# Low parts of the two query projections' weights formed on GpSimd instead of VectorE

## The chip, the cores and the metric

The kernel runs on one core of one Trainium2 chip. The metric is the device time of one execution in microseconds (us); a figure for a kernel is the median of several executions. The trace behind the profile comes from one more execution, taken by the hardware profiler. TensorE's granted clock is given as a share of full speed: 1.00 is 2.4 GHz, 0.50 is 1.2 GHz.

## The reference

Four layers run one after the other on 256 tokens of width 1024, in float32: a gated-MLP mixer and a chunked attention, each with a convolutional feed-forward; then an "even" layer (two attentions and a feed-forward) and an "odd" layer, followed by a final norm. The change lies in the odd layer's attention:

```
q, k, v, iq, ik, iw = split(h @ w_in)          # q: 16 heads x 64, k and v: 4 heads x 64
q, k, iq, ik = rope(...)                       # rotation of each half head
score = sum over 8 index heads of iw * relu(iq . ik)
idx   = top_k(score, 64)                       # for each query, 64 keys of the 256
o     = softmax(q . k[idx]) @ v[idx]           # 4 query heads share a key head
x     = x + g_m * (o @ w_out)
```

Behind it the odd layer has a mixture of 8 experts, two for each token, each with gate, up and down matrices of 1024 x 1408.

## The kernel before, in words

**Split weights.** A float32 product is computed as three TensorE products of rounded operands. A weight block `r`, loaded into a tile `raw`, is split by `split` (line 245): ScalarE rounds it to `hi` (tile `wh`, line 261), and VectorE forms the rest, `lo = r - hi` (tile `wl`, line 262). `unit` (line 265) cuts a loaded block of 128 x 2048 into two splits of 128 x 1024. `mm3` (lines 277 to 280) makes the three products: line 278 and line 279 use the weights' high and low parts with the activation's high part, line 280 the weights' high part with the activation's low part. The tags `wh` and `wl` have 4 buffers each, `raw` has 4.

**Token-major projections.** `tok_out` (line 373) multiplies the 256 tokens (two tiles of 128, `m` = 0 and 1) by a weight in units of half the inputs by `cols` outputs. The sums of both token tiles stand in two PSUM banks; after the second unit of a column block `evac` takes them out. For the projections named `m` in the trace there are two such banks (tag `m`).

**The odd layer's attention, `dsa`** (line 1068 on), in the order of the code: `tok_out` of the index queries (`o_iq`); `tok_out` of keys, index key and index weights (`o_ki`), whose evacuation rotates the keys (lines 885 to 901), transposes them (lines 909 and 779) and copies them (lines 910, 782, 784); then the key selection, `choose(1)` and `choose(0)` side by side: scores by TensorE (line 1110), relu by ScalarE (line 1114), weighted sums `sc` by VectorE (lines 1120 and 1122), the causal mask (1125), 8 rounds of "the eight largest, then strike them out" (lines 1129 and 1130), and the mask `sel` (1132 and 1133). Then the values (`o_v`), then `query(0)` and `query(1)`: each is a `tok_out` of two units of `o_q`, that is four splits of 128 x 1024, with an evacuation `ev_q` that rotates (lines 885 to 895), transposes (779) and stores the queries. Then four attention groups, which need the queries and `sel`, the output projection (`wo`), and the experts.

**Order.** Each engine runs its own queue in order. The queues are laid out when the kernel is built, by a list scheduler with estimated durations: what stands first in the code goes first when several instructions are ready, and later ones fill what it takes for gaps. So subtractions of line 262 for `o_q` stand in VectorE's queue before, between and behind the instructions of the selection. GpSimd, before the change, only computes the norms' inverse roots (lines 307, 949, 950), on 128 x 1 tiles.

Of the kernel before, what the change touches and what calls it, by code (L numbers as in the profile page):

```python
# [13 lines left out]
ALU = mybir.AluOpType  # L14
# [144 lines left out]
def tile_net(ctx: ExitStack, tc: tile.TileContext, a: dict, out: bass.AP):  # L159
    nc = tc.nc  # L160
    V, S, G, PE = nc.vector, nc.scalar, nc.gpsimd, nc.tensor
# [14 lines left out]
    def t_keep(tag, n, bufs, dt=F32):  # L176
        return keep.tile([P, n], dt, tag=tag, name=tag, bufs=bufs)

    def t_part(tag, n, bufs, dt=F32):
        return part[0].tile([P, n], dt, tag=tag, name=tag, bufs=bufs)  # L180

    def psd():
        return ps_p.tile([P, 512], F32, tag="d", name="d", bufs=4)
# [7 lines left out]
    def sm(tag, n, bufs=4):  # L191
        return t_keep("s_" + tag, n, bufs)

    def a8(dt=F32):
        return t_keep("a8", 2048, 6, dt)

    def xn_(dt=F32):
        return t_keep("xn", D, 2, dt)
# [43 lines left out]
    turn = [0]  # L242
    fine = [FINE]

    def split(r, where=None):

        n = r.shape[-1]
        if where == "a8":
            t = a8(F32R)
            hi, lo = t[:, 0:n], t[:, 1024:1024 + n]  # L250
        else:
            turn[0] += 1
            if where and turn[0] % 2:
                hi, lo = (t_part(g, 1024, where, F32R)[:, 0:n] for g in ("whx", "wlx"))
            else:
                hi, lo = (t_keep(g, 1024, WB, F32R)[:, 0:n] for g in ("wh", "wl"))
        parts = 2 if fine[0] > 0 and n > 512 else 1
        fine[0] -= 1
        for i in range(parts):
            cs = slice(i * n // parts, (i + 1) * n // parts)  # L260
            S.activation(hi[:, cs], r[:, cs], AF.Copy)  # L261
            V.tensor_tensor(lo[:, cs], r[:, cs], hi[:, cs], op=ALU.subtract)  # L262
        return hi, lo

    def unit(src, k, where=None, loaded=None):

        r = load(src) if loaded is None else loaded
        n = r.shape[-1] // k
        per = k if k * n <= 1024 else -(-k // 2)
        w = []  # L270
        for k0 in range(0, k, per):
            kk = min(per, k - k0)
            hi, lo = split(r[:, k0 * n:(k0 + kk) * n], where)
            w += [(hi[:, i * n:(i + 1) * n], lo[:, i * n:(i + 1) * n]) for i in range(kk)]
        return w

    def mm3(ps, lh, ll, rh, rl, start, stop):
        PE.matmul(ps, lh, rh, start=start, stop=False)  # L278
        PE.matmul(ps, lh, rl, start=False, stop=False)  # L279
        PE.matmul(ps, ll, rh, start=False, stop=stop)  # L280
# [30 lines left out]
    def new_xt():  # L311
        return tuple(a8(F32R).rearrange("p (k t) -> p k t", k=NK) for _ in range(2))
# [56 lines left out]
    def tok_out(xt, src, cols, evac, psx=None, where=None, loaded=(), ready=()):  # L369

        xh, xl = xt
        for c in range(src.shape[0] // 2):
            ps = [(psx or psd)()[:, 0:cols] for _ in range(2)]
            for kh in range(2):
                u = 2 * c + kh
                w = ready[u] if u < len(ready) else unit(src[u], 4, where, loaded[u] if u < len(loaded) else None)
                for m in range(2):
                    ts = slice(m * P, (m + 1) * P)
                    for k in range(4):
                        kk = 4 * kh + k  # L380
                        mm3(ps[m], xh[:, kk, ts], xl[:, kk, ts], *w[k], kk == 0, kk == NK - 1)
            for m in range(2):
                evac(m, c, ps[m])
# [119 lines left out]
    def ada_all(nm):  # L503
        while any(t[0] == nm for t in ada_todo):
            ada_step()
# [251 lines left out]
    def half(t, hd, idx=None):  # L757
        return t[(hd % 2) * 64:(hd % 2) * 64 + 64, hd // 2 if idx is None else idx, :]
# [145 lines left out]
    def tr_copy(src, dst, m, scale=1.0):  # L904

        n = src.shape[1] // P
        ps = pst()
        for c in range(n):
            PE.transpose(ps[:, c * P:(c + 1) * P], src[:, c * P:(c + 1) * P], ident)
        S.activation(dst[:, :, m * P:(m + 1) * P], ps[:, 0:n * P].rearrange("p (k t) -> p k t", k=n),  # L910
                     AF.Copy, scale=scale)
# [167 lines left out]
    def dsa():  # L1079
        xt = ahead[2]  # L1080
        ib, kk = a8(), a8(F32R)
        oT = new_xt()
        ikT = ib[:, 0:256].unsqueeze(1)
        iw = ib[:, 256:272].rearrange("p (m d) -> p m d", m=2)
        iqT = ib[:, 512:1536].rearrange("p (k t) -> p k t", k=4)
        sel = t_part("sel", 512, 1, F32R).rearrange("p (m t) -> p m t", m=2)
        kh, kl = (kk[:, i * D:(i + 1) * D].rearrange("p (k t) -> p k t", k=4) for i in range(2))
        vv = ib[:, 1536:2048].rearrange("p (m d) -> p m d", m=2)
        def ev_iq(m, c, ps):
            tr_copy(rotate(ps, m, 8), iqT, m)  # L1090

        tok_out(xt, a["o_iq"], 512, ev_iq)

        def ev_ki(m, c, ps):
            tr_copy(rotate(ps[:, 256:320], m, 1, dup=2), ikT, m)
            V.tensor_scalar(iw[:, m, :], ps[:, 320:328], float(8 ** -0.5 * 64 ** -0.5), None, op0=ALU.mult)
            stack(rotate(ps[:, 0:256], m, 4, dup=2), m, kh, kl)

        tok_out(xt, a["o_ki"], 328, ev_ki)

        def choose(m):

            nk = (m + 1) * P
            sc = t_part("sc", T, 2)[:, 0:nk]
            first = True
            for h0 in (0, 1, 4, 5):
                ps = psd()
                for i in range(2):
                    hd = h0 + 2 * i
                    PE.matmul(ps[:, i * nk:(i + 1) * nk], half(iqT, hd)[:, m * P:(m + 1) * P],  # L1110
                              half(ikT, hd, 0)[:, 0:nk], start=True, stop=True)
                yield
                rl = t_part("pT", 512, 4)
                S.activation(rl[:, 0:2 * nk], ps[:, 0:2 * nk], AF.Relu)
                yield
                for i in range(2):
                    hd = h0 + 2 * i
                    r1, w1 = rl[:, i * nk:(i + 1) * nk], iw[:, m, hd:hd + 1]
                    if first:
                        V.tensor_scalar(sc, r1, w1, None, op0=ALU.mult)  # L1120
                    else:
                        V.scalar_tensor_tensor(sc, r1, w1, sc, op0=ALU.mult, op1=ALU.add)
                    first = False
                yield
            V.tensor_tensor(sc[:, m * P:], sc[:, m * P:], m_caus, op=ALU.add)
            yield
            for _ in range(8):
                mx = sm("top", 8)
                V.max(mx, sc)
                V.match_replace(sc, mx, sc, -3e38)  # L1130
                yield
            V.tensor_scalar(sel[:, m, 0:nk], sc, -3e38, NEG, op0=ALU.not_equal, op1=ALU.mult)
            V.tensor_tensor(sel[:, m, m * P:nk], sel[:, m, m * P:nk], m_caus, op=ALU.add)

        def ev_v(m, c, ps):
            S.activation(vv[:, m, :], ps, AF.Copy)

        qs = []

        def query(c, ready=()):  # L1140
            for _ in range(2):
                q = xn_(F32R) if c == 0 else t_part("qs", D, 2, F32R)
                qs.append(q.rearrange("p (k t) -> p k t", k=4))

            def ev_q(m, _, ps):
                for o, q in zip(rotate(ps, m, 8, parts=True), qs[2 * c:]):
                    stack(o, m, q, scale=0.125)

            tok_out(xt, a["o_q"][2 * c:2 * c + 2], 512, ev_q, psm, ready=ready)

        def group(g, psx):
            attend(stacked(qs, kh, kl, 0, lambda hd: g), lambda hd, kb: vv[:, kb, g * 64:(g + 1) * 64],
                   None, oT, g, psx,
                   rmask=lambda m: sel[:, m, 0:(m + 1) * P])

        ada_all("o")
        rows_out("o", mod_scale("o", 4, "o_norm_ffn_2"))
        together(choose(1), choose(0))
        tok_out(xt, a["o_v"], 256, ev_v, psm)
        query(0)  # L1160
        g_m = spread("o", 2)
        ready = [unit(a["o_q"][2 + u], 4) for u in range(READY)]
        for step in ORD:
            if step == "q":
                query(1, ready)
            else:
                group(int(step), psd if step in PSD else psm)
        plan()
        out_proj(oT, a["wo3"], g_m)
# [293 lines left out]
```

## Time and profile before

| | before |
|---|---|
| median of 3 runs | 1533.95 us (1530.49 to 1535.28) |
| profiled execution | 1537.47 us |
| its span in the trace | 1535.5 us |
| mean granted TensorE clock | 0.981 |
| busy: TensorE matmuls, VectorE, ScalarE, GpSimd | 1460.7, 1219.9, 932.1, 16.5 us |

The span runs from the first to the last instruction of the trace; the profiled execution took 1.97 us more than its span, and 3.5 us more than the median of the runs without a profile. Busy times are sums over the whole span; a stage has to be read from its own windows.

### The profile page before, as it was taken

The numbers are of one execution on the slowest core, as the hardware profiler recorded it, in microseconds if no ns is written. First come the engines' busy times: TensorE is split into PE (matmuls) and PEld (weight loads), VectorE is DVE, ScalarE is ACT, GpSimd is POOL, SyncE is SP. The second block draws the span as 40 slices with busy tenths as digits, with TensorE's granted clock in tenths as the row PEclk, the third lists the DMA queues.
The fourth block names the chain that finished last, engine by engine and source line by source line (L and its number), as shares of the span: only waits on it lengthen the run. The fifth ranks groups of instructions, "written<-read, shape, count | busy, mean of one in ns | idle before, by whom it ended". The sixth has DMA issues, their size and how long they took to land.

```text
span 1535.5 us, 23191 instructions
## 1 busy us (share of the span) xinstructions
PE 1460.7 (95%) x8916; PEld 1284.8 (84%) x8916; DVE 1219.9 (79%) x2074; ACT 932.1 (61%) x1559; POOL 16.5 (1%) x26
## 2 busy tenths in 40 slices
PE   6999999999999999899899999989799999999996
PEld 5889998899899889788699998778688888888875
DVE  7589887776698777776898875886788889888996
ACT  7656555555575546565654443545577777777774
POOL 0000000000000000000000000000000000000000
PEclk9999999999999999999999999999899999999999
DMA  8658666454387664262488881431489988899894
GB/s 311 218 195 325 226 244 219 149 199 162 134 295 281 220 219 165 83 255 105 164 329 329 322 309 63 180 138 34 152 319 332 335 328 320 319 346 332 294 352 155
DMA packets 55148, 363.05 MB, mean 236 GB/s; under 512 B 6526, under 2 KB 6886, under 8 KB 16630
## 3 DMA queue, kind: packets, MB, share of 16 engines
q1 hardware_dynamic: 55030, 361.50, 65.3%
q8 instruction: 72, 1.18, 0.3%
q14 instruction: 46, 0.38, 0.1%
HBM read 360.37 MB, written 1.10 MB: 235 GB/s over the span
## 4 chain that ended last, share of the span: by engine, by line
PE 82%; DVE 8%; ACT 5%; DMA 4%; issue 1%; POOL 0%; SPq 0%; POOLq 0%; ACTq 0%; DVEq 0%
PE d L278 12%; PE d L279 12%; PE d L280 12%; PE m L279 10%; PE m L280 9%; PE m L278 9%; PE t L280 2%; PE t L279 2%; PE t L278 2%; DMA raw<-in_fin_dram 2%; PE d L745 1%; DVE wl L262 1%; PE t L323 1%; PE t L734 1%; PE t L1259 1%
## 5 line engine op out<-in xcount | busy, mean ns | idle before, releaser
L262 DVE TENSOR_TENSOR wl<-raw,wh 128x1024 fp32r<-128x1024 f32 (+4 forms) x342 | 363.1, 1069 | 71.8 <-ACT wh L261 70.4
L261 ACT ACTIVATE wh<-raw 128x1024 fp32r<-128x1024 f32 (+4 forms) x342 | 315.5, 932 | 121.8 <-PE m L280 30.4
L262 DVE TENSOR_TENSOR wlx<-raw,whx 128x1024 fp32r<-128x1024 f32 (+2 forms) x231 | 258.9, 1123 | 46.1 <-ACT whx L261 45.2
L261 ACT ACTIVATE whx<-raw 128x1024 fp32r<-128x1024 f32 (+2 forms) x231 | 224.0, 975 | 59.1 <-PE m L279 17.1
L278 PE MATMUL d<-wh,a 128*128 128x512 f32 (+4 forms) x448 | 167.9, 376 | 8.6 <-ACT a L344 8.6
L279 PE MATMUL d<-wl,a 128*128 128x512 f32 (+4 forms) x448 | 165.9, 372 | 0.4 <-DVE wl L262 0.4
L280 PE MATMUL d<-wh,a 128*128 128x512 f32 (+4 forms) x448 | 165.5, 371 | 0.2
L279 PE MATMUL m<-a,wh 128*128 128x256 f32 x496 | 141.5, 285 | 0.0
L278 PE MATMUL m<-a,wh 128*128 128x256 f32 x496 | 141.4, 285 | 0.0
L280 PE MATMUL m<-a,wl 128*128 128x256 f32 x496 | 141.3, 285 | 0.0
L500 DVE SCALAR_TENSOR_TENSOR raw<-raw,silu_c 128x1024 f32<-128x1024 f32 x96 | 116.0, 1218 | 4.5 <-DMA raw<-in_e_ada_dram 2.9
L278 PE MATMUL d<-a,th 128*128 128x512 f32 x264 | 107.2, 406 | 6.7 <-ACT th L565 6.6
L279 PE MATMUL d<-a,th 128*128 128x512 f32 x264 | 105.4, 399 | 0.0
L278 PEld LDWEIGHTS d<-wh,a 128*128 128x128 f32 x448 | 86.5, 193 | 22.6 <-ACT a L344 10.9
L261 ACT ACTIVATE a<-raw 128x1024 fp32r<-128x1024 f32 (+1 forms) x72 | 70.0, 986 | 53.1 <-PE d L280 48.1
L279 PE MATMUL d<-wlx,a 128*128 128x512 f32 (+2 forms) x272 | 99.8, 367 | 1.1 <-DVE wlx L262 1.1
L278 PE MATMUL d<-whx,a 128*128 128x512 f32 (+2 forms) x272 | 99.7, 367 | 0.6 <-ACT a L669 0.6
L262 DVE TENSOR_TENSOR a<-raw,a 128x1024 fp32r<-128x1024 f32 (+1 forms) x72 | 81.0, 1132 | 23.7 <-ACT a L261 23.5
L280 PE MATMUL d<-a,tl 128*128 128x512 f32 x264 | 99.6, 404 | 0.0
L280 PE MATMUL d<-whx,a 128*128 128x512 f32 (+2 forms) x272 | 99.4, 365 | 0.0
L279 PEld LDWEIGHTS d<-wl,a 128*128 128x128 f32 x448 | 86.6, 193 | 13.1 <-DVE wl L262 1.6
L280 PEld LDWEIGHTS d<-wh,a 128*128 128x128 f32 x448 | 86.0, 192 | 13.3 <-DVE a L347 1.9
(367 smaller groups left out, 3499.6 us busy)
## 6 DMA issues: line engine op xcount, KB each, us to landing
raw<-in_fin_dram SPq DMA_DIRECT2D x66, 1024.0 KB, 5.1
raw<-in_x_dn_dram SPq DMA_DIRECT2D x40, 1024.0 KB, 6.4
raw<-in_fdn_dram SPq DMA_DIRECT2D x33, 1024.0 KB, 5.1
raw<-in_x_gate_dram SPq DMA_DIRECT2D x32, 1024.0 KB, 6.2
raw<-in_x_up_dram SPq DMA_DIRECT2D x32, 1024.0 KB, 6.8
raw<-in_e_ada_dram SPq DMA_DIRECT2D x24, 1024.0 KB, 5.6
raw<-in_o_ada_dram SPq DMA_DIRECT2D x24, 1024.0 KB, 7.1
raw<-in_wo_dram SPq DMA_DIRECT2D x16, 1024.0 KB, 5.7
```

The costliest lines, as they stand in the source:

```text
L261: S.activation(hi[:, cs], r[:, cs], AF.Copy)
L262: V.tensor_tensor(lo[:, cs], r[:, cs], hi[:, cs], op=ALU.subtract)
L278: PE.matmul(ps, lh, rh, start=start, stop=False)
L279: PE.matmul(ps, lh, rl, start=False, stop=False)
L280: PE.matmul(ps, ll, rh, start=False, stop=stop)
L323: PE.transpose(ps[:, c * P:(c + 1) * P], src[:, c * P:(c + 1) * P], ident)
L500: V.scalar_tensor_tensor(rr, rr, 1.0, silu_c, op0=ALU.mult, op1=ALU.mult, accum_out=t[:, i:i + 1])
L734: PE.transpose(pt[:, b * P:(b + 1) * P], s2[:, b * P:(b + 1) * P], ident)
L745: PE.matmul(ps[:, i * 64:(i + 1) * 64], pT[:, b * P:(b + 1) * P], vv(hd, kb), start=kb == 0, stop=kb == m)
L1259: PE.matmul(ps, gr[:, m, :], t[:, m, cs], start=i == 0, stop=i == 3)
```

## The change

The engine that forms low parts becomes a variable, `low[0]`, which is VectorE everywhere except while `query` runs its `tok_out`: there it is GpSimd. So the eight subtractions of 128 x 1024 for `o_q` (two units for each `query`, two splits for each unit) are issued to GpSimd. All else, the rounding on ScalarE included, stays where it was in the code.

```
+    low = [V]
...
             S.activation(hi[:, cs], r[:, cs], AF.Copy)
-            V.tensor_tensor(lo[:, cs], r[:, cs], hi[:, cs], op=ALU.subtract)
+            low[0].tensor_tensor(lo[:, cs], r[:, cs], hi[:, cs], op=ALU.subtract)
...
+            low[0] = G
             tok_out(xt, a["o_q"][2 * c:2 * c + 2], 512, ev_q, psm, ready=ready)
+            low[0] = V
```

## Rows read from the trace of the kernel before

**Rows 1.** First lines of the page: busy time, share of the span, instructions.
```profile
PE 1460.7 (95%) x8916; PEld 1284.8 (84%) x8916; DVE 1219.9 (79%) x2074; ACT 932.1 (61%) x1559; POOL 16.5 (1%) x26
```
**Rows 2.** Busy us by window; last columns: granted clock, DMA share, GB/s.
```profile
1002.60:1006.20 3.60, 3.57 (x8) 2.84 (x9) 3.60 (x5) 0.00 (x0) 0.00 (x0) 0.50 0.34 84
...
1150.00:1200.00 50.00, 50.00 (x241) 42.06 (x240) 43.80 (x49) 39.01 (x48) 0.00 (x0) 1.00 0.93 333
```
**Rows 3.** What TensorE waited for, 975 to 1023: us, times, longest.
```profile
PE m L279 <- DVE wl L262: 6.4, 1, 6.4
```
**Rows 4.** Timeline of TensorE: start, duration, line, op, tiles, shape, count.
```profile
981.73 0.27 PE L909 MATMUL t<-cst,rt 128*128 128x128 f32 x1
...
990.18 0.40 PE L278 MATMUL m<-wh,a 128*128 128x512 f32 x1
...
995.65 0.61 PE L278 MATMUL m<-wh,a 128*128 128x512 f32 x2
1002.63 0.80 PE L279 MATMUL m<-wl,a 128*128 128x512 f32 x1 [6.37 <-DVE wl L262]
...
1003.65 0.63 PE L278 MATMUL m<-wh,a 128*128 128x512 f32 x1
1004.08 0.63 PE L279 MATMUL m<-wl,a 128*128 128x512 f32 x1
...
1022.24 0.40 PE L280 MATMUL m<-wh,a 128*128 128x512 f32 x1
```
**Rows 5.** Timeline of VectorE over the selection and the first query evacuation.
```profile
978.66 1.22 DVE L262 TENSOR_TENSOR wl<-raw,wh 128x1024 fp32r<-128x1024 f32 x1
979.79 0.75 DVE L901 TENSOR_TENSOR rt<-rt 128x256 f32<-128x256 f32 x2
...
980.91 0.36 DVE L901 TENSOR_TENSOR rt<-rt 128x64 f32<-128x64 f32 x2
...
983.86 1.22 DVE L262 TENSOR_TENSOR wl<-raw,wh 128x1024 fp32r<-128x1024 f32 x1
...
991.22 0.42 DVE L1129 MAX8 s_top<-sc 128x8 f32<-128x256 f32 x1
...
1001.35 1.23 DVE L262 TENSOR_TENSOR wl<-raw,wh 128x1024 fp32r<-128x1024 f32 x1
1002.48 0.30 DVE L1133 TENSOR_TENSOR sel<-sel,cst 128x128 fp32r<-128x128 f32 x1
...
1007.18 0.69 DVE L885 TENSOR_TENSOR rt<-m,cos 128x512 f32<-128x512 f32 x1 [0.42 <-PE m L280]
...
1008.12 0.41 DVE L887 TENSOR_TENSOR rt<-m,sin 128x256 f32<-128x256 f32 x1
```
**Rows 6.** Timeline of ScalarE: roundings of `o_q`, and the index key's copy.
```profile
977.10 2.01 ACT L261 ACTIVATE wh<-raw 128x1024 fp32r<-128x1024 f32 x2 [1.26 <-PE d L280]
...
981.01 1.06 ACT L261 ACTIVATE wh<-raw 128x1024 fp32r<-128x1024 f32 x1 [1.74 <-PE m L280]
...
982.45 0.27 ACT L910 ACTIVATE a<-t 128x128 f32<-128x128 f32 x1
...
990.66 1.05 ACT L261 ACTIVATE wh<-raw 128x1024 fp32r<-128x1024 f32 x1
```
**Rows 7.** Timeline, GpSimd beside VectorE, early and in the even layer.
```profile
42.30 0.15 DVE L304 TENSOR_SCALAR s_ms<-s_ms 128x1 f32<-128x1 f32 x1
...
42.37 1.22 DVE L262 TENSOR_TENSOR wl<-raw,wh 128x1024 fp32r<-128x1024 f32 x1
...
42.53 1.46 POOL L307 TENSOR_TENSOR s_r<-s_ms,mhalf 128x1 f32<-128x1 f32 x1 [29.06 <-DVE s_ms L304]
...
621.73 0.55 POOL L950 TENSOR_TENSOR s_r<-s_ms,mhalf 128x1 f32<-128x1 f32 x1 [194.07 <-DVE s_ms L945]
621.84 0.69 DVE L452 TENSOR_TENSOR h<-h,d 128x512 f32<-128x512 f32 x1 [0.26 <-PE d L280]
```
**Rows 8.** What the DMA queue waited for, 980 to 1035.
```profile
SPq L239 <- DVE wl L262: 32.2, 4, 12.2
```

## Prediction

> **What bounds the kernel now.** I read the page first: TensorE is busy for 95% of the span, VectorE for 79%, and GpSimd for 1% [rows 1]. That only says who has room on average. The windows say where the time is lost: among the experts, which fill the span from about 1100 on, TensorE is busy for 50.00 of 50 us at full clock [rows 2], so what is gained ahead of them should move them forward as a block, and nothing that this change does can shorten them. Next I read the list of waits around the key selection. It has one large entry: TensorE stood 6.4 us for line 279, which reads a low part, until VectorE had made it [rows 3].
>
> The timelines show how that came about. TensorE began the first query projection at 990.18, finished its first unit (24 products, 0.228 us apart), issued two more at 995.65, and then stood until 1002.63 [rows 4]. The low part that it wanted is the one VectorE made at 1001.35; its rounded half had been ready since ScalarE's instruction at 981.01 ended, at 982.07 [rows 5, 6]. So the subtraction was ready 19 us before it ran: it stood in VectorE's queue behind the selection, whose eight rounds start at 991.22 and whose last instruction ends at 1002.78 [rows 5]. The stall has a second price. Behind it the granted clock is 0.50, that is 1.2 GHz, until 1006.2 [rows 2], and products come 0.43 us apart instead of 0.228 [rows 4]: nine of them, 9 x 0.20 = 1.8 us. Together 6.4 + 1.8 = 8.2 us is what this place could give at most.
>
> **The change part by part.** It takes eight subtractions off VectorE and puts them on GpSimd. Two of them stand ahead of the selection, at 978.66 and 983.86, one at 1001.35 inside its last instructions, the rest behind [rows 5].
>
> *TensorE without the stall.* The third low part can be formed from 982.07 on, long before it is wanted at 996.1 (995.65 and two products). The first query's two units then end at 996.1 + 22 x 0.228 = 1001.1. The next query's products need the PSUM bank of the first, which is free when VectorE has rotated out of it: from the start of line 885 to the end of line 887 took 1007.18 to 1008.53, 1.35 us [rows 5]. VectorE comes to that when the selection is over: 1002.78, less 1.13 us for the subtraction at 1001.35, less what the two early ones give back. They took 1.13 us each, but the selection's start hangs on ScalarE and TensorE as well (ScalarE's copy of the index key came at 982.45, behind a rounding that started at 981.01 [rows 6]), so I count 0.8 of 2.3 us. The bank is free at 1002.78 - 1.13 - 0.8 + 1.35 = 1002.2, and TensorE waits 1.1 us for it: the stall does not vanish, it moves to "rotation behind selection". Gain so far 8.2 - 1.1 = 7.1, say 7 us.
>
> *What a subtraction costs on GpSimd.* The trace has none. The nearest rows: from below VectorE's own, 1.22 us; from above, GpSimd's 128 x 1 operation takes 0.55 us where VectorE's takes 0.15 us [rows 7], and 0.55 / 0.15 x 1.22 = 4.5 us. The ends are far apart; I take their geometric mean, 2.35 us, which is an estimate. At that price GpSimd's queue is never late: the first three are done by about 985 to 988, the others follow ScalarE's roundings, which come when TensorE has released a buffer. The Trainium skill, GPSIMD Engine Reference, section 3.1, measures a two-input operation on 128 x 2048 at 4497 ns on GpSimd against 2293 ns on VectorE, and advises VectorE for such work; half of it, 2.25 us as an estimate, would make the sum below 0.2 us better, and no run here shows it.
>
> *GpSimd and VectorE side by side.* This is where the gain can leak. GpSimd's 128 x 1 operation, 0.55 us elsewhere, took 1.46 us when a subtraction with two SBUF operands ran on VectorE from 42.37 to 43.59: it ended 0.40 us after that. Beside an instruction of VectorE that has one operand in PSUM it took 0.55 us [rows 7]. So GpSimd is held up by such an instruction. Whether VectorE is held up while GpSimd streams, no row shows, since GpSimd never streamed. Bounds: below, VectorE never waits, 0 us. Above, each of the three subtractions that fall between 978 and 986 stops it for its whole length: the first starts at 978.1, when its rounding ends [rows 6], and stops the pair of line 901 that now comes at 978.7; the second and third stop the next ones, among them the index key's pair at 980.91 [rows 5], on which the selection hangs. That is 3 x 2.35, less the 1.13 us that line 262 took there before, less 0.45 us of slack (the transposed key was there at 982.0, its copy came at 982.45 [rows 4, 6]): 5.5 us. I take two of three, since VectorE's rotations alternate between PSUM and SBUF operands and the third can fall beside the former: 2 x 2.35 - 1.13 - 0.45 = 3.1, say 3 us later for the selection and for TensorE, whose score products and all behind them move with it. The fourth rounding comes at 990.66 [rows 6], so the later subtractions fall into the eight rounds, whose instructions read one tile; there I count nothing. The Trainium skill, SBUF — State Buffer, section "Who interferes with whom", says that a VectorE instruction with two SBUF inputs and a GpSimd instruction that reads SBUF exclude each other for the whole instruction, whichever comes first. Rows 7 agree for the one direction; by that rule the delay of 3 us stands, and without it the sum would be 7 us.
>
> *Clock.* TensorE would idle about 3 us ahead of the scores. Whether the clock then falls as it did behind 6.4 us I can't read; I take no cost, and 1.8 us as the other end.
>
> *Queues and waits.* GpSimd's queue holds nothing else here (the next inverse root comes behind the output projection). The DMA queue waited for line 262 four times, 32.2 us in all [rows 8], to refill `raw`; it now waits for GpSimd, which is done with the later units earlier than VectorE was, and the loads concerned (`wo`) are wanted only behind the attention groups.
>
> **Sum.** 8.2 - 1.1 - 3.1 = 4.0 us faster. The profiled execution would take 1537.5 - 4.0 = 1533.5 us; the runs without a profile have their median 3.5 us below it, so I forecast 1533.95 - 4.0 = 1530.0 us.
>
> **Rivals.**
>
> *B, VectorE is not held up.* Only GpSimd waits, as in rows 7. Gain 7 us: 1527.0, with 1525.5 to 1528.5 from the slot wait and the two early subtractions. For it: the only direction that the trace shows. Against it: something shared that stops one side.
>
> *C, GpSimd is slow.* At 4.5 us a subtraction, two held-up places give 2 x 4.5 - 1.6 = 7.4 us, gain -0.4: 1534.4; with a third 1538.9. Decides from 4.3 us on. For it: the ratio of the small operations. Against: that ratio is of fixed costs.
>
> *D, the selection's rounds are held up too; slower.* If the largest-eight and strike-out instructions are stopped as well, the three subtractions that become ready in 991 to 1000 (fourth to sixth) each add 2.35 us to a chain of VectorE on which the next bank hangs: 7.05 us more, 4.0 - 7.05 = 3 us slower, 1537.0. It turns to a loss when 1.7 of the three are waited for in full. Against it: these instructions read one tile from SBUF, as does the one in rows 7 that held nothing up.
>
> *E, given back.* The block of the experts doesn't move forward, because its weights come no sooner: the DMA engines are at 0.93 there [rows 2]. 1533.95. Against: TensorE has no gap in that window.
>
> **How the numbers follow.** Chances: forecast 0.45, B 0.25, C 0.10, D 0.12, E 0.08. A change under 0.3%, 4.6 us, can't be told from none here. Faster by more: nearly all of B (0.24), a third of the forecast's case (0.16), 0.02 of the rest: 0.42. Slower by more: half of D, half of C, 0.01 of E: 0.12. Within: 0.46. The range runs from B's best, 1525.5, to between C and D, 1535.5; the upper half of C and D, a sliver of B and the spread of a median lie outside, under 0.2. The likeliest case alone has 1528.5 to 1531.5.
>
> **What would show it.** Right: eight subtractions on GpSimd of some 2.35 us; no 6.4 us wait for a low part; a wait of about 1 us for a PSUM bank at the second query's start; a full clock between 1000 and 1006; instructions of line 901 on VectorE that last 1 to 2 us longer; scores some 3 us later; attention groups 4 us earlier. B: line 901 unchanged and the groups 7 us earlier. C: subtractions over 4 us. D: stretched lines 1129 and 1130. Wrong altogether if the scheduler lays VectorE's or TensorE's queue out in another order, so that the selection moves or queries are rotated inside it.

## The result, and the profile after

| | before | after |
|---|---|---|
| median of 7 runs, side by side | 1533.95 us (1530.49 to 1538.36) | 1541.45 us (1538.87 to 1544.8) |
| profiled execution, its span | 1537.47, 1535.5 us | 1542.14, 1540.3 us |
| mean granted clock | 0.981 | 0.979 |

The ratio is 1.0051, with a 95% interval of 1.0035 to 1.0066: slower by half a per cent, outside the predicted range and of the other sign. Lines of `kernel.py` behind the first edit have moved: 262 is 264 now, 885 to 901 are 887 to 903, 779 is 781, 1110 is 1112; from 1132 on, 1132 is 1134.

GpSimd's timeline after (start, duration, line, operation, tiles, shape, count) shows the eight subtractions at some 2.4 us each, and that they come in two groups: two ahead of the scores, six from 995 on.

```profile
975.36 4.86 POOL L264 TENSOR_TENSOR wl<-raw,wh 128x1024 fp32r<-128x1024 f32 x2 [18.22 <-ACT wh L263]
995.15 2.48 POOL L264 TENSOR_TENSOR wl<-raw,wh 128x1024 fp32r<-128x1024 f32 x1 [14.93 <-ACT wh L263]
999.57 2.41 POOL L264 TENSOR_TENSOR wl<-raw,wh 128x1024 fp32r<-128x1024 f32 x1 [1.94 <-ACT wh L263]
1003.45 4.83 POOL L264 TENSOR_TENSOR wl<-raw,wh 128x1024 fp32r<-128x1024 f32 x2 [1.47 <-ACT wh L263]
1008.89 2.42 POOL L264 TENSOR_TENSOR wl<-raw,wh 128x1024 fp32r<-128x1024 f32 x1 [0.61 <-ACT wh L263]
1013.64 2.39 POOL L264 TENSOR_TENSOR wl<-raw,wh 128x1024 fp32r<-128x1024 f32 x1 [2.33 <-ACT wh L263]
```

VectorE's timeline after: read the durations against the same instructions of before. The rotation's pair on 128 x 256 took 0.75 us [rows 5] and takes 4.60; line 1134 (the mask) takes 3.67 for two, which took 0.29 and 0.23 before; line 891 takes 1.47 and 2.75 where line 889 took 0.69 on average before. Each overlaps a row of the fence above.

```profile
975.90 4.60 DVE L903 TENSOR_TENSOR rt<-rt 128x256 f32<-128x256 f32 x2
...
1004.70 3.67 DVE L1134 TENSOR_SCALAR sel<-sc 128x256 fp32r<-128x256 f32 x2
...
1010.39 1.47 DVE L891 TENSOR_TENSOR rt<-rt 128x512 f32<-128x512 f32 x1
...
1013.83 2.75 DVE L891 TENSOR_TENSOR rt<-rt 128x512 f32<-128x512 f32 x1
```

The eight rounds between them are not stretched, though two subtractions run beside them. VectorE's groups by line, 970 to 1020 us (busy us, then mean ns; 421 ns is the mean before as well):

```profile
L1131 DVE MAX8 s_top<-sc 128x8 f32<-128x256 f32 x8 | 3.4, 421 | 0.0
```

What TensorE waited for, 960 to 1100 us (us in total, times, longest): the 6.4 us wait for a low part [rows 3] is gone, and three others stand in its place: that for `s` of line 897 (the queries' parts) was 1.7 us before, those for `rt` of line 903 (the keys) and of line 889 (a PSUM bank that the rotation still reads) are new.

```profile
PE t L781 <- DVE s L897: 4.5, 4, 2.1
PE t L781 <- DVE rt L903: 3.5, 1, 3.5
...
PE m L280 <- DVE rt L889: 1.5, 1, 1.5
```

TensorE's timeline after, from the last product of the key projection to the router behind the attention:

```profile
974.77 0.31 PE L282 MATMUL d<-wh,a 128*128 128x328 f32 x1
...
980.65 1.08 PE L781 MATMUL t<-cst,rt 128*128 128x128 f32 x4 [3.52 <-DVE rt L903]
...
983.37 3.09 PE L1112 MATMUL d<-a 64*128 64x256 f32 x10
986.39 1.11 PE L781 MATMUL t<-cst,rt 128*128 128x128 f32 x4
...
987.65 5.82 PE L1112 MATMUL d<-a 64*128 64x256 f32 x22
...
997.96 0.40 PE L280 MATMUL m<-wh,a 128*128 128x512 f32 x1
...
1098.17 0.60 PE L1245 MATMUL m<-pk,cst 128*128 128x8 f32 x2 [2.68 <-DVE pk L1215]
```

And the clock in windows at the 3.52 us hole, as the time in which TensorE stood is called below, and behind it (the column behind the busy times):

```profile
977.00:981.00 4.00, 0.48 (x4) 0.39 (x3) 4.00 (x7) 0.00 (x0) 3.22 (x2) 0.84 0.72 301
981.00:984.00 3.00, 3.00 (x14) 2.68 (x13) 2.42 (x8) 0.87 (x2) 0.00 (x0) 0.50 0.92 317
...
992.00:996.00 4.00, 4.00 (x18) 3.68 (x17) 3.52 (x13) 2.10 (x4) 0.85 (x1) 0.50 0.86 263
996.00:1000.00 4.00, 4.00 (x24) 3.65 (x24) 4.00 (x21) 1.71 (x3) 2.06 (x2) 0.91 0.06 26
```

TensorE stood 3.52 us for the keys' rotation, and its clock was then 0.50 from 981 to 996, though it was busy without a gap. The last 22 score products took 5.82 us; where the clock was 1.00 (run e2 below) 22 of them took 3.09.

Three marks on TensorE's timeline make the account, since they hold in every run: A, the last 128 x 328 product; B, the first 128 x 512 product of the queries; C, the first product behind the wait for `pk`. Before, A and C are

```profile
977.65 0.31 PE L280 MATMUL d<-wh,a 128*128 128x328 f32 x1
...
1094.15 0.59 PE L1241 MATMUL m<-pk,cst 128*128 128x8 f32 x2 [2.68 <-DVE pk L1211]
```

and B is at 990.18 [rows 4]. So A to B was 12.53 us and is 997.96 - 974.77 = 23.19: 10.66 us lost ahead of the queries. B to C was 103.97 and is 100.21: 3.76 us gained behind it. Together 6.9 us slower in this stage. In these two profiles A itself stands 2.9 us earlier after the change, and what follows C takes 0.8 us longer, so the span is only 4.8 us longer.

### The profile page after: what moved, and what is told of

Its sections match the earlier page's. It is cut to its first block, busy times and chain, and to the rows that moved or that the text cites. A ratio compares the mean times of both kernels' runs of the same rounds, so it can differ in the third digit from the quotient of the medians.

```text
span 1540.3 us, 23189 instructions
## 1 busy us (share of the span) xinstructions
PE 1464.8 (95%) x8916; PEld 1287.1 (84%) x8916; DVE 1221.6 (79%) x2066; ACT 933.3 (61%) x1559; POOL 36.0 (2%) x34
## 4 chain that ended last, share of the span: by engine, by line
PE 81%; DVE 8%; ACT 5%; DMA 4%; issue 1%; POOL 0%; SPq 0%; POOLq 0%; ACTq 0%; DVEq 0%
PE d L280 12%; PE d L281 12%; PE d L282 12%; PE m L281 9%; PE m L282 9%; PE m L280 9%; PE t L282 2%; PE t L281 2%; PE t L280 2%; DMA raw<-in_fin_dram 1%; PE d L747 1%; PE t L325 1%; PE t L736 1%; DVE wl L264 1%; PE t L1263 1%
## 5 line engine op out<-in xcount | busy, mean ns | idle before, releaser
L264 DVE TENSOR_TENSOR wl<-raw,wh 128x1024 fp32r<-128x1024 f32 (+4 forms) x334 | 353.4, 1066 | 72.4 <-ACT wh L263 71.2
L282 PEld LDWEIGHTS d<-wh,a 128*128 128x128 f32 x448 | 85.7, 191 | 13.1 <-DVE a L349 1.6
L280 PEld LDWEIGHTS m<-a,wh 128*128 128x128 f32 x496 | 94.7, 191 | 1.8 <-issue 0.7
```

The costliest lines, as they stand in the source:

```text
L264: low[0].tensor_tensor(lo[:, cs], r[:, cs], hi[:, cs], op=ALU.subtract)
```

## The experiments

Theory C: a subtraction on GpSimd holds some of VectorE's instructions for its whole length, and what TensorE waits for is late by that. Rival O: the list scheduler laid the queues out in another order (the first key transposes of line 781 now stand behind 16 value products on TensorE instead of 24, and ScalarE rounds the third block behind the scores), and the order costs the time. All marks are in one table; the medians of before, in the same sessions, were 1533.4 (e1 to e4), 1533.35 (e5 to e8) and 1533.98 (e9 to e12). Marks come from the one profiled execution of each run, times from 6 to 12 executions; the profiled one of e7 was the slowest of its twelve; u0 and u1 are the first query's two units. In all fourteen profiles TensorE does the same 91 products from A to B and the same 534 from B to C, and what follows C takes 441.1 to 445.5 us (before: 441.3).

| run | median us | ratio to before, 95% | A to B | B to C |
|---|---|---|---|---|
| before | | 1 | 12.53 | 103.97 |
| after | 1541.45 | 1.0051 [1.0035, 1.0066] | 23.19 | 100.21 |
| e1 ghost | 1554.04 | 1.0126 [1.0091, 1.016] | 26.41 | 109.47 |
| e2 memset | 1525.35 | 0.9953 [0.9933, 0.9973] | 12.08 | 96.06 |
| e3 quarters | 1530.49 | 0.9987 [0.9967, 1.0008] | 13.92 | 98.93 |
| e4 u0 on VectorE | 1537.1 | 1.0013 [0.9992, 1.0034] | 17.99 | 100.73 |
| e5 same, quarters | 1529.99 | 0.9972 [0.9959, 0.9985] | 13.10 | 101.67 |
| e6 u1 only, quarters | 1533.91 | 0.9999 [0.9983, 1.0015] | 13.10 | 102.54 |
| e7 VectorE, early | 1534.9 | 1.0005 [0.9993, 1.0017] | 12.08 | 105.37 |
| e8 product in PSUM | 1536.44 | 1.0014 [0.9998, 1.0029] | 11.95 | 106.68 |
| e9 u0 in quarters | 1533.26 | 1.0003 [0.9988, 1.0018] | 13.92 | 101.33 |
| e10 u0 whole | 1537.7 | 1.0024 [1.0006, 1.0041] | 23.25 | 98.38 |
| e11 PSUM, quarters | 1534.48 | 1.0002 [0.9986, 1.0019] | 11.96 | 106.90 |
| e12 e5 with PSUM | 1532.4 | 1.0 [0.9985, 1.0016] | 11.98 | 103.63 |

**e1, the contention alone.** VectorE forms all low parts again, and the queues of every engine but GpSimd's are those of the kernel before. GpSimd repeats the eight subtractions into a tile that nothing reads.

```
+            V.tensor_tensor(lo[:, cs], r[:, cs], hi[:, cs], op=ALU.subtract)
+            if low[0] is G:
+                G.tensor_tensor(silu_c[:, cs], r[:, cs], hi[:, cs], op=ALU.subtract)
```

> All low parts are formed on VectorE as before, and every instruction queue but GpSimd's is the one of before; GpSimd forms the eight low parts of o_q a second time, into a tile that nobody reads. Theory C (contention: a streaming GpSimd subtraction and a VectorE instruction with two SBUF operands, or a fast one, keep each other out for a whole instruction): VectorE's rotations ahead of the selection stretch as after the change, some 2 to 4 us in all, the selection and TensorE come later by that, and the execution is 3 to 8 us slower than before. Rival O (order: the loss comes from the new order of the queues, and GpSimd's work itself costs nothing): no difference from before within 1.5 us, and no stretched VectorE instruction.

It took 1.26% longer, 19 to 21 us, far more than the 3 to 8 expected, with nothing changed in the order. VectorE's timeline (262 is 264 here, the lines of the rotation are 4 above those of before): the same pair of rotations takes 5.04 us, a later one 5.07, and a subtraction on VectorE itself takes 3.06 us where it takes 1.22 alone.

```profile
970.59 3.06 DVE L264 TENSOR_TENSOR wl<-raw,wh 128x1024 fp32r<-128x1024 f32 x1
973.57 5.04 DVE L905 TENSOR_TENSOR rt<-rt 128x256 f32<-128x256 f32 x2
...
1016.48 5.07 DVE L899 TENSOR_TENSOR s<-rt,s 128x256 f32<-128x256 f32 x2
```

As after the change, the clock adds to it: TensorE stood 5.9 us for the pair, and behind that its clock was 0.50, in this window for instance:

```profile
980.00:998.00 18.00, 18.00 (x67) 15.24 (x66) 12.54 (x41) 7.14 (x15) 0.30 (x1) 0.50 0.45 148
```

**e2, the order alone.** TensorE's, VectorE's, ScalarE's and SP's queues are those of after. GpSimd fills the low part with zeros instead of subtracting, so the low parts of the query weights are left out of the result.

```
+            if low[0] is V:
+                V.tensor_tensor(lo[:, cs], r[:, cs], hi[:, cs], op=ALU.subtract)
+            else:
+                G.memset(lo[:, cs].bitcast(F32), 0.0)
```

> The queues of TensorE, VectorE, ScalarE and the DMA queue are those of after the change; in place of each of the eight subtractions GpSimd writes zeros into the low part, which reads nothing from SBUF (so the low parts of the query weights are left out of the result). Theory C: the pair of rotations (line 903) takes 0.75 us instead of 4.60, TensorE's 3.5 us wait ahead of the key transposes shrinks below 1 us, the clock stays at 1.00 through the scores, and the execution is 4 to 8 us faster than before, 12 to 15 us faster than after. Rival O: the transposes stand ahead of the value products all the same, so it is as slow as after, some 7 us slower than before.

8 us faster than before. O falls as the cause: in the very order of after, the stage is 8.4 us shorter than before, and the clock is 1.00 from 970 to 1000. Timelines of e2, GpSimd's first, then VectorE's (the fill is also shorter than a subtraction and doesn't wait for ScalarE, so this is a bound for the idea, not a version of it):

```profile
975.96 0.95 POOL L267 MEMSET wl<- 128x1024 f32 x1 [2.62 <-PE m L284]
...
995.21 0.95 POOL L267 MEMSET wl<- 128x1024 f32 x1 [0.41 <-PE m L284]
```

```profile
976.54 0.76 DVE L906 TENSOR_TENSOR rt<-rt 128x256 f32<-128x256 f32 x2
...
993.24 0.42 DVE L1137 TENSOR_SCALAR sel<-sc 128x256 fp32r<-128x256 f32 x2
...
995.68 0.69 DVE L894 TENSOR_TENSOR rt<-rt 128x512 f32<-128x512 f32 x1
```

The pair at 976.54 starts beside a fill and takes its usual 0.76 us, and the sum at 995.68 starts beside another and takes its usual 0.69: GpSimd's writes hold neither, its reads did. (The mask at 993.24 has no fill beside it; 0.42 us for two is its length undisturbed.)

**e3, the same work in smaller pieces.** Queues of after; each subtraction on GpSimd is cut into four of 128 x 256.

```
+            k = 1 if low[0] is V else 4
+            for p in range(k):
+                ps_ = slice(cs.start + p * (cs.stop - cs.start) // k, cs.start + (p + 1) * (cs.stop - cs.start) // k)
+                low[0].tensor_tensor(lo[:, ps_], r[:, ps_], hi[:, ps_], op=ALU.subtract)
```

> As after the change, with the same queues on the other engines, but each GpSimd subtraction is cut into four of 128 x 256. Theory C: an exclusion lasts only as long as one instruction, some 0.65 us, so the pair of line 903 takes 1.5 to 2.5 us instead of 4.60, TensorE's hole ahead of the key transposes is 0.5 to 1.5 us, and if that leaves the clock at 1.00 the execution is between 5 us faster and 1 us slower than before. Rival O: as slow as after, about 7 us slower than before, since the order is the same.

Some 11 us faster than after, and not to be told from before. GpSimd works longer (0.84 us a piece on average, 3.3 us a subtraction), but an instruction of VectorE now waits for a piece: the pairs take 1.36 and 1.77 us in place of 4.60, TensorE's holes at line 784 are 0.27 and 0.75 us, and the clock stays at 1.00.

**e4 and e5, the first unit back on VectorE.** Its two subtractions stand on VectorE, the other six on GpSimd; whole in e4, in quarters (the loop of e3) in e5.

```
-            low[0] = G
+            low.extend(([V, V, G, G], [G, G, G, G])[c])
...
-            low[0].tensor_tensor(lo[:, cs], r[:, cs], hi[:, cs], op=ALU.subtract)
+            (low.pop(0) if low else V).tensor_tensor(lo[:, cs], r[:, cs], hi[:, cs], op=ALU.subtract)
```

> The first unit's two low parts go back to VectorE, the other six stay on GpSimd; ahead of the selection the queues are those of before. Theory C: no stretched rotation ahead of the selection, no hole, the clock at 1.00 until the queries, and the 6.4 us wait for a low part gone; but the two sel instructions (line 1134) and the query rotations (line 891) still stretch by 3 to 5 us in all. Faster than before by 0 to 5 us. If the loss sat in the later six subtractions instead: slower than before by 3 us or more.

> The first projection's first unit (two subtractions) stays on VectorE, the other six go to GpSimd, each cut into four of 128 x 256. Theory C (a whole subtraction on GpSimd holds VectorE for its length; a piece holds it for a piece's length): the stretched instructions of the earlier run of this order with whole subtractions (the rotation's pair 1.93 us, the selection's two 2.23 and 2.33 us) fall to under 1.3 us, TensorE has no hole over 0.6 us ahead of the scores, the clock is at 0.9 or more from 980 to 1010, and the kernel takes 1527 to 1531 us, 3 to 7 us faster than before. Rival O (the order of the queues decides): the same as with whole subtractions, 1535 to 1539 us.

e4 misses its gain: one subtraction still fell beside the rotation's pair (1.93 us), TensorE had a hole of 0.93 us, and the clock was 0.76, 0.50 and 0.72 in the three windows of 5 us from 980. In quarters the hole is 0.52 us, the clock is 1.00 from 965 to 1000, and e5 is the one complete version whose interval lies below 1: 0.28% faster, at the edge of what can be told, and the best of several that were tried. It can't be told from e3 (0.9967 to 1.0008).

**e6, only what stood behind the selection.** The second unit's two subtractions of the first query go to GpSimd in quarters, the rest stays on VectorE (`[V, V, G, G], [V, V, V, V]`).

> Only the two subtractions that stood behind the selection (the second unit of the first projection) go to GpSimd, in quarters; the other six stay on VectorE. Theory C: with two subtractions in small pieces there is little to hold; the 6.4 us wait for a low part is gone or moved to a bank wait under 3 us, and the kernel takes 1527 to 1531 us. Rival O: whatever stands on GpSimd, the time follows the place of the key transposes in TensorE's queue; where that is as in the kernel before, the gain ahead of the scores is nothing and only the stall behind the selection changes, 1530 to 1534 us.

The 6.4 us wait is gone, and the time is as before: a miss for C. In its place TensorE waits 2.0 us for the mask, 1.3 us for a PSUM bank, and runs at a clock of 0.80 to 0.86 from 1000 to 1010.

**e7, no GpSimd at all.** The first query's two units are split on VectorE ahead of the selection, and the value projection is moved ahead of it too.

```
-            low[0] = G
+            low[0] = V
...
+        tok_out(xt, a["o_v"], 256, ev_v, psm)
+        first = [unit(a["o_q"][u], 4) for u in range(2)]
         together(choose(1), choose(0))
-        tok_out(xt, a["o_v"], 256, ev_v, psm)
-        query(0)
+        query(0, first)
```

> Nothing on GpSimd: the first projection's two units are split on VectorE ahead of the selection instead of behind it. Theory C: the stall of 6.4 us was a matter of VectorE's order alone, so it goes without contention: no instruction of VectorE is stretched, the low parts are there when TensorE wants them, the bank wait behind the selection is 0 to 3 us, and the kernel takes 1526 to 1531 us, about as the run in which GpSimd only fills with zeros (1525.35). Rival: the two or three subtractions set ahead of the selection (1.13 to 1.3 us each) make the selection and the rotations later by as much, and the gain is under 3 us, 1531 to 1535 us.

No gain, as the rival had it. The stall for a low part is gone; the selection starts 15.72 us behind A in place of 13.57, its mask holds TensorE for 2.8 us and the bank for 1.1, and the clock is 0.50 from 1005 to 1010. Here, moving the subtractions earlier on VectorE only moved the stall; how much of the delay is the value projection's, no run tells.

**e8, which instructions are held.** Whole subtractions on GpSimd, but the rotation keeps its first product in PSUM, so that its sum has one operand in SBUF and one in PSUM. (The scheduler's order is another one again.)

```
-        V.tensor_tensor(hv(t1), hv(ps), bc(rope["cos"], 0, 64), op=ALU.mult)
...
+        V.tensor_tensor(hv(ps), hv(ps), bc(rope["cos"], 0, 64), op=ALU.mult)
+        t1 = ps
```

> The changed kernel, whole subtractions on GpSimd, but the rotation keeps its first product in PSUM, so that none of its instructions reads two operands from SBUF. Theory C by operands (only an instruction of VectorE with two SBUF operands, or the fast one-operand form, is held while GpSimd reads SBUF): the rotation's last two instructions take under 1 us each though GpSimd streams beside them, TensorE's hole ahead of the scores is under 1 us, the clock stays up there, the two instructions that form the mask are still stretched to 2 us or more, and the kernel takes 1527 to 1536 us, at least 5 us less than the changed kernel. Rival (any VectorE instruction is held): the pair still takes over 2.5 us and the time stays at 1539 to 1544 us.

Timelines of e8, GpSimd's and then VectorE's:

```profile
973.75 7.05 POOL L264 TENSOR_TENSOR wl<-raw,wh 128x1024 fp32r<-128x1024 f32 x3 [18.27 <-ACT wh L263]
...
996.05 4.69 POOL L264 TENSOR_TENSOR wl<-raw,wh 128x1024 fp32r<-128x1024 f32 x2 [0.66 <-ACT wh L263]
```

```profile
974.05 0.75 DVE L905 TENSOR_TENSOR rt<-d,rt 128x256 f32<-128x256 f32 x2
...
978.00 0.75 DVE L905 TENSOR_TENSOR rt<-d,rt 128x256 f32<-128x256 f32 x2
978.84 2.30 DVE L1124 TENSOR_SCALAR sc<-pT,a 128x256 f32<-128x256 f32 x2
...
996.21 4.62 DVE L1136 TENSOR_SCALAR sel<-sc 128x256 fp32r<-128x256 f32 x2
```

Both pairs lie inside GpSimd's 7.05 us and take 0.75 us each: with one operand in PSUM nothing is held. The hole ahead of the scores is gone, the clock is 1.00 from 975 to 995, A to B is 11.95 us. What is still held is the form with one SBUF tile and a scalar, lines 1124 and 1136: 2.30 us for two of the weighted sums, 4.62 us for the two of the mask, and TensorE stood 5.2 us for it.

The Trainium skill, SBUF — State Buffer, section "Who interferes with whom", says that VectorE contends with GpSimd's reads when it has two SBUF inputs, and with GpSimd in some fast forms of one input, among them `tensor_scalar`; that others do not contend; and that the blocked side waits for the whole instruction. These rows agree: 4.60 us against 0.75 for the same pair by where its operand lies, 4.62 us against 0.42 for the mask, 421 ns against 421 for the eight largest, 0.76 us beside a fill that reads nothing. No row has a fast form beside a fill.

**e9 and e10, the loss in two parts.** Queues of after. In e9 only the two subtractions ahead of the scores are cut in quarters, in e10 only the other six. (`[4, 4, 1, 1], [1, 1, 1, 1]` and `[1, 1, 4, 4], [4, 4, 4, 4]` pieces.)

> The changed kernel with the first unit's two subtractions alone (those ahead of the selection) in quarters; the other six stay whole, and all queues but GpSimd's are those of the changed kernel. It splits the loss: in the changed kernel's trace the hole ahead of the scores is 3.5 us and the half clock behind it costs the scores 8.91 - 4.76 = 4.2 us and the products around them 1.4 us, 9.1 us together; behind the selection the held instructions cost 1.5 + 2.8 us of waits. Theory C with the clock: hole under 1.1 us, clock at 0.9 or more from 977 to 1000, 7 to 9 us less than the changed kernel, 1532 to 1535 us. Rival (the half clock is not the hole's doing, or the time comes back at the selection): under 4.5 us less, 1537 us or more.

> The complement: the first unit's two subtractions whole, the other six in quarters. Theory C with the clock: the hole of some 3.5 us ahead of the scores and the half clock behind it stay, the mask's two instructions fall from 3.67 us to under 1.5 us, and the kernel takes 1537 to 1540 us, 2 to 4 us less than the changed kernel. Rival as in the run before: 4.5 to 9 us less.

e9 is 8.2 us below after, e10 3.8 us, both inside what C with the clock had said; together 12.0, and e3, which does both, is 11.0 below. The two parts add up. (Between the profiles, A to C is 8.2 us shorter in e9 and 1.8 in e10, so the second part is the less certain.) TensorE's hole ahead of the scores is in e9, at its longest, and in e10:

```profile
983.73 0.63 PE L784 MATMUL t<-cst,rt 128*128 128x128 f32 x4 [0.75 <-DVE rt L906]
```

```profile
977.72 1.09 PE L784 MATMUL t<-cst,rt 128*128 128x128 f32 x4 [3.54 <-DVE rt L906]
```

The granted clock in windows of e9 (from 975) and of e10 (from 980) tells how the first part works:

```profile
975.00:1000.00 25.00, 23.56 (x146) 20.54 (x145) 24.70 (x94) 12.07 (x21) 15.95 (x12) 1.00 0.66 233
```

```profile
980.00:990.00 10.00, 10.00 (x39) 7.88 (x38) 6.05 (x18) 3.92 (x9) 0.00 (x0) 0.50 0.37 133
```

With the hole cut to at most 0.75 us the clock stays at 1.00 and A to B is 13.92 us; with the hole of 3.54 us it falls to 0.50 and A to B is 23.25.

**e11 and e12, what is left.** e8's rotation with all eight in quarters, and with the first unit on VectorE besides.

> The rotation with its product in PSUM, and all eight subtractions on GpSimd in quarters: the queues are those of the earlier run with the product in PSUM but for GpSimd's. Theory C: what was left there, the mask's first instructions held for 4.62 us, falls to under 1.5 us; the 5.2 us wait of TensorE for the mask falls to under 2.5 us; 1530 to 1534 us, 3 to 6 us less than with whole subtractions. Rival (that wait is of the order, not of the hold): 1535 to 1538 us.

> The best version so far (first unit on VectorE, six in quarters on GpSimd) with the rotation's product in PSUM as well; the order of the queues changes with it. If holds were all that was left, it is 1 to 3 us faster than that version, 1527 to 1529 us; if the order of the queues decides now, it can go either way by 3 us, and the fast version without this edit stays the best.

e11 brings the mask's first two instructions from 4.62 to 1.20 us and the wait for the mask from 5.2 to 3.2 us, and its median is 2 us below e8's, short of the 3 to 6 expected; e12 doesn't beat e5. In both, A to B is at 12 us, as short as with the fill, and B to C is 106.90 and 103.63, against 103.97 before: in this order TensorE's queue has attention products that read the mask ahead of the second query's, so it stands 3 us for the selection's end. That the order costs these 3 us is argued, since no run changes it alone.

## Why the prediction was wrong, by its own steps

- **"I take no cost, and 1.8 us as the other end"**, the clock ahead of the scores, is the step that failed. The hole itself was foreseen ("about 3 us", measured 3.52). But A to B grew by 10.66 us, of which 3.52 is the hole; the other 7.1 us are the half clock, which held from 981 to 996. Fifteen us at half speed are 7.5 us of lost work, which fits. e9 and e10 show it: without and with the hole, 13.92 and 23.25 us, all queues but GpSimd's the same. A term taken at zero was nearly as large as the whole gain of 8.2.
- **"There I count nothing"**, for the later subtractions, is the second. The eight rounds were not held (rival D's mechanism is wrong: 421 ns before and after), but the subtractions came later than supposed, since ScalarE's third rounding moved from 981.01 [rows 6] to 994.01, and ran on to the mask and to the rotations of the queries, which were held. TensorE's wait for the queries' parts grew from 1.7 to 4.5 us: 2.8 us. By e10 cutting these six is worth 3.8 us between the medians, 1.8 between the profiles.
- **The stall of 6.4 us and its 1.8 us of clock** were sized rightly: in e2, where nothing is held, B to C is 103.97 - 96.06 = 7.9 us shorter, against 8.2.
- **The bank wait** was 1.5 us, against 1.1. **GpSimd's subtraction** took 2.4 us, against 2.35, so rival C had no ground; that the mean of two bounds as far apart as 1.22 and 4.5 came so near is luck.
- **VectorE held up**: not two places by one subtraction each, but one pair by two subtractions back to back (4.60 us, 3.85 more than before). So rival B fell. The delay to TensorE has the predicted size, 3.5 us against 3.1, but reached it by another way, the transposes of the keys and not the index key, so the agreement is in part luck. And the 0.55 us row of [rows 7] could not show what an operand in PSUM does, since GpSimd's instruction began there 0.11 us before VectorE's; e8 shows it.
- **The order** did change, as the last line of "what would show it" had warned, and by e2 it wasn't the loss; it bears on where the holds struck, since the key transposes that waited stood ahead of value products that could have run; but e1, in the order of before, had its hole at the same transposes.
- **Rival E**, that the experts give a gain back, fell as well: behind C each profile takes 441.1 to 445.5 us, so most of what is lost or gained ahead of C is passed on. The longest is e2's, which gave back some 4 us of it.

The sum with measured terms: - 8.2 + 1.5 (bank) + 3.5 (hole) + 7.1 (clock) + 2.8 (held rotations) = 6.7 us slower, against 6.9 between A and C and 7.5 between the medians.

Why e6 and e11 gain less than a single wait would give can be read from their traces. In all fourteen profiles B to C is the time that TensorE stood, plus half of the time that it was busy at 0.50, plus 85.5 to 86.7 us. In e6 TensorE stood 13.1 us against 15.5 before, because the waits for the mask and the bank took the place of the 6.4 us, and lost 2.7 us to the clock against 2.9. In e11 it stood 15.2 us against 16.9 in e8, but lost 6.0 us to the clock against 3.6: the clock fell a second time, at 1028, among the attention groups. What stays open is why the clock falls and rises when it does, and how much of the wait at the selection's end is the order's.

## What to carry to other kernels

Moving work to an idle engine wasn't free here: look for VectorE instructions with two SBUF operands, or with one and a scalar, beside the new GpSimd ones. Cutting GpSimd's instructions into pieces makes a hold last a piece; in e3 that took the loss away, but left no gain that can be told. A hole in TensorE must be priced with the clock behind it; here 3.5 us of waiting cost 7.1 us more. And a stall behind a chain such as this selection may only move: in e7 the work stood earlier on the same engine and nothing was gained.

## What the runs showed of the hardware

The clock behind a hole doesn't follow the hole's length. Before, 6.37 us of standing were followed by less than 4 us at 0.50 [rows 2], with 128 x 512 products behind it [rows 4]; after, 3.52 us were followed by some 15 us at 0.50, with score products on 64 rows and transposes behind it. In e4 a hole of 0.93 us was followed by 10 us at 0.50; in e3, e5 and e9 holes up to 0.75 us ahead of the scores left the clock at 1.00, and so did 1.93 us of standing for a bank in e3, with 128 x 512 products on both sides. What decides was not tried.

The hold goes both ways: in e1, where both engines had two-operand work at once, GpSimd's first three subtractions took 8.16 us together, against 7.05 in e8, and VectorE's own took 3.06 us, against 1.22.
